# Residual tiles fetched two ahead in three buffers, and products ordered by weight half within a chunk, in a two-block float32 transformer kernel

## The chip, the cores and the metric

The kernel runs on one core of one Trainium2 chip. The metric is the device time of one execution in microseconds (us); less is better. The time before is the median of three executions, 2883.99 us (2881.13 to 2885.41).

## What is computed

Two transformer-like blocks run one after the other on a sequence of 512 tokens of width 2048, all in float32. Cut to what matters here:

```python
def reference(x, mem, ..., c_2, ctx_2, ...):
    x = first_block(x, mem, ...)      # one layer: state-space scan, differential attention, memory attention
    return second_block(x, c_2, ctx_2, ...)   # two layers on 512 tokens beside a context of 256 tokens

def first_block(x, mem, ...):
    h = rmsnorm(x, norm_pre); proj = h @ w_in            # 5120 columns
    ...
    mix = jnp.concatenate([y_s, y_d, y_x], -1) @ w_out
    x = x + rmsnorm(mix, norm_post)                      # the residual that the change is about

def second_block(x, c, ctx, ...):
    for l in range(2):
        h  = rmsnorm_2(x,  norm_g[l]) * (1 + scale) + shift
        hc = rmsnorm_2(xc, norm_g[l]) * (1 + scale_c) + shift_c
        ...                                              # both go through w_in[l], attention, pooling, a Fourier mix, w_out[l]
        x  = x + gate * out
        xc = xc + gate_c * outc                          # not in the last layer
    return rmsnorm_2(x, final_norm_g)
```

## The kernel before

**Layout.** Activations lie transposed in SBUF: 16 tiles of 128 features by n tokens (n is 512 for the sequence, 256 for the memory and the context). A product of the large weights with them is made by `gemm` (line 515): one output tile of 128 features by n tokens gathers in one PSUM tile `mm` over 2048 input features. Weights come in chunks of 512 input by 128 output features (`raw`, 256 KB, by a DMA on the SP queue). One output tile takes four chunks (two in the product with `w_glu`).

**Products in two halves.** For accuracy every float32 operand is split in a high half, rounded by ScalarE (`whi` of a weight chunk, `hh` of an activation tile), and a low half, the rest, which VectorE subtracts (`wlo`, `hl`). A product of two operands is three matmuls: high by high, high weight by low activation, low weight by high activation. `mm3` (line 328) issues them in that order, and `gemm` calls it for each of the four 128-row pieces of a chunk: 12 matmuls, of which the third is the first that needs `wlo`. There are 912 chunks.

**The weight pipeline.** `wload` (475) puts the load of a chunk on SP into one of four `raw` buffers; a `raw` buffer is free when VectorE has made the `wlo` of the chunk that lay there. `wsplit` (481) issues the cast to `whi` on ScalarE and, a little later, the subtraction to `wlo` on VectorE. Both have four buffers each, and run three chunks ahead of the products.

**The order of the work.** All engines run their instructions in the order of the program text, and the program text is made by a planner: `tick` (432), called between matmuls and with a clock that advances by the estimated cost of each matmul, lets pieces of other work ("background" generators) issue their next instructions. So evaluation of finished tiles, attention, norms and the adaptive-norm products (`adaw`, `tp`) stand between the products on every engine. In `gemm` before, `tick` is called after each of the four pieces of a chunk.

**Block 1's residual.** After the product with `w_out`, the background generator `post` in `block2` (line 1716) makes the new residual stream, tile by tile for k from 0 to 15: it loads `xr` (a tile of the kernel's input `xT`, 256 KB), multiplies `X[k]` (the tile `mx`) by the norm factor `B`, adds `xr`, writes the tile to DRAM (`x1d`) and sums its squares into `acc`. The load of tile k is issued just ahead of the multiplication and the addition of tile k, into one of two buffers. Beside this, PE makes the products of the context (256 tokens) with `w2_in0`, layer 0 of block 2: the stage from about 1023 to 1185 us of the trace.

Of the kernel before, what the change touches and what calls it, by code (L numbers as in the profile page):

```python
# [22 lines left out]
N = 512  # L23
# [191 lines left out]
class Build:  # L215
# [299 lines left out]
    def gemm(self, name, mt, H, n, order, ahead=None):  # L515
        while len(self.live["mm"]) > 1 and (self.pmx is None or self.live["mx"]):
            self.tick(0.5)
        if len(self.live["mm"]) < 2:
            ps = self.t(self.pmm, "mm", [128, n], bufs=2)
            self.live["mm"].append(ps.tensor.name)  # L520
        else:
            ps = self.t(self.pmx, "mx", [128, n])
            self.live["mx"].append(ps.tensor.name)
        ks = lambda a: [order[a] * 4 + kk for kk in range(4)] if a < len(order) else []
        for a, ci in enumerate(order):
            if ahead is not None and a == 2:
                self.spawn(self.split_ahead(ahead))
            hi, lo = self.wget((name, mt, ci, n))
            while lo.tensor.name not in self.split_w:
                self.tick(0.3)  # L530
            while any(k not in H.ok for k in ks(a)):
                self.tick(0.3)
            H.need(ks(a) + (ks(a + 1) if self.wi > 1 else []))
            for kk in range(4):
                s = slice(kk * 128, kk * 128 + 128)
                self.mm3(ps, (hi[:, s], lo[:, s]), H[ci * 4 + kk],
                         a == 0 and kk == 0, a == len(order) - 1 and kk == 3)
                if kk < 3 or a < len(order) - 1:
                    self.tick()
        return ps  # L540

# [1138 lines left out]
    def block2(self):  # L1680
        nc, I = self.nc, self.I
        o4r = (2, 3, 0, 1)

        es_c = ExitStack()
        cxp = self.pool("cx1", es_c, bufs=1)
        es = ExitStack()
        pp = self.pool("post1", es, bufs=1)
        self.ada_gap = 1.3
        X = [None] * 16
        acc = self.t(pp, "acc", [128, N])  # L1690
        hc = [self.t(cxp, f"cx{k}", [128, NC]) for k in range(KT)]
        HC = Lazy(self, NC, lambda Hk, k: self.conv(Hk, hc[k], bias=self.adav[0][:, 1, k:k + 1]), False)
        last = []

        def ev(m, ps):
            X[m] = self.t(self.xp, f"mx{m}", [128, N])
            self.act(X[m], ps, AF.Copy, scale=self.vec("norm_post", m))
            sq = acc if m == 0 else self.t(pp, "sq", [128, N], bufs=2)
            self.act(sq, ps, AF.Square)
            self.over(ps)  # L1700
            yield
            if 0 < m < 15:
                self.add(acc, acc, sq)
            last[:] = [sq]

        fs, fc = [], None
        for m, ps in self.gemms("w_out", range(16), self.H, N, o4r, HC):
            fs.append(self.spawn(ev(m, ps)))
            if m == 11:
                self.ada_until("G0_1")  # L1710
            if m == 2:
                fc = self.spawn(self.ctx_rows(hc, pp, lambda k: I["ctxT"][:, k], 0, HC))
        self.ada_gap = 4
        HX = Lazy(self, N, lambda Hk, k: self.conv(Hk, X[k], bias=self.adav[0][:, 0, k:k + 1]), False)

        def post():
            yield 12
            while self.alive([fc, *fs]):
                yield 0
            B0 = yield from self.g_bcast([acc, last[0]], N, D)  # L1720
            B = self.t(pp, "B", [128, N], bufs=2)
            yield
            nc.scalar.copy(B, B0)
            self.over(B0)
            yield
            xr = []
            for k in range(16):
                xr.append(self.t(pp, "xr", [128, N], bufs=2))
                self.load(xr[k], I["xT"][:, k])
                if k == 0:  # L1730
                    yield
                self.mul(X[k], X[k], B)
                self.add(X[k], X[k], xr[k])
                yield 3.0
                nc.sync.dma_start(out=self.x1d[k], in_=X[k])
                sq = acc if k == 0 else self.t(pp, "sq", [128, N], bufs=2)
                self.act(sq, X[k], AF.Square)
                yield 0.3
                if 0 < k < 15:
                    self.add(acc, acc, sq)  # L1740
            B0 = yield from self.g_bcast([acc, sq], N, D)
            B = self.t(pp, "B", [128, N], bufs=2)
            yield
            nc.scalar.copy(B, B0)
            self.over(B0)
            yield
            for k in list(range(8, 16)) + list(range(8)):
                self.stt(X[k], X[k], self.G0_0[:, k:k + 1], B, ALU.mult, ALU.mult)
                HX.ok.add(k)
                yield 2.2  # L1750
                if k >= 8:
                    HX.need([k])

        fp = self.spawn(post())


        es_kv = ExitStack()
        kvp = self.pool("ckv", es_kv, bufs=1, side="right")
        es_p = ExitStack()
        self.ps_ = self.pool("psSc", es_p, bufs=1, space=PSUM)  # L1760
        self.pmx = self.pool("pmx", es_p, bufs=1, space=PSUM)
        self.layer(0, NC, HC, cxp, "cx", kvp, None, lambda: (self.join(fp), es.close()), None,
                   lambda _: self.lead(self.gemms("w2_in0", range(8, 12), HX, N, o4r), self.LEAD[3]))
        es_c.close()
        es_p.close()
        self.pmx = None
        self.ps_ = self.pool("psS", bufs=1, space=PSUM)


        self.ada_gap = 2  # L1770
        self.layer(0, N, HX, self.xp, "mx", kvp, self.x1d, None, self.next_kv,
                   lambda H: self.lead(self.gemms("w2_in1", range(8, 12), H, NC, o4r), self.LEAD[3]))
        es_kv.close()


        es_kv = ExitStack()
        kvp = self.pool("ckv1", es_kv, bufs=1, side="right")
        HC, HX1, fin, es_o = self.next_h

        def early():  # L1780
            yield from fin
            for k in range(8, 16):
                HX1.need([k])
                yield 0.7
        fe = self.spawn(early(), now=False)
        es_t = ExitStack()
        tp_ = self.pool("ckt", es_t, bufs=1)
        self.scp, self.scw, self.scb = tp_, NC, 4
        self.ckv = self.kv(1, NC, HC, o4r, kvp, "c", False, self.next_kv)
        kvs = self.lead(self.gemms("w2_in1", range(8, 12), HX1, N, o4r), self.LEAD[3])  # L1790
        self.join(fe, *self.kvf)
        es_t.close()
        es_o.close()
        self.layer(1, N, HX1, self.xp, "mx", kvp, self.x2d, None, kvs)
        es_kv.close()
# [407 lines left out]
```

## Time and profile before

| What | Before |
|---|---|
| median of 3 runs | 2883.99 us (2881.13 to 2885.41) |
| the profiled execution: its own time | 2885.97 us |
| its span, first to last instruction | 2884.2 us |
| mean granted TensorE clock | 0.978 of full speed |
| PE (matmuls) busy | 2740.9 us, 95%, 17390 instructions |
| PEld (weight loads) busy | 2279.8 us, 79% |
| DVE (VectorE) busy | 1664.8 us, 58% |
| ACT (ScalarE) busy | 1213.8 us, 42% |
| POOL (GpSimd) busy | 168.3 us, 6% |
| DMA moved | 412.73 MB, mean 143 GB/s |

A share of busy time is a mean over stages that differ; what ends a wait is read stage by stage. All instructions carry line 210 (L210), since one helper records every operation, so groups go by the names of tiles: `mm<-hh,wlo` is a matmul into `mm` with moving operand `hh` and weights `wlo`, `wlo<-raw,whi` the subtraction on VectorE, `mx<-mx,xr` the residual addition. SPq is the DMA queue of SyncE, on which all loads and stores of this program are issued. An entry such as "[3.0 <-DMA xr<-xT]" at the end of a row is idle time of the engine just before the instruction, and what ended it. PEclk is the granted clock of TensorE as a share of full speed.

### The profile page before, as it was taken

The page shows a single profiled execution, that of the slowest core. Times are in us where ns is not written, and L with a number is a line of the kernel's source. Part 1 is how long each engine was busy: PE and PEld are TensorE (multiplying, and loading weights), DVE is VectorE, ACT ScalarE, POOL GpSimd, SP SyncE. Part 2 cuts the span into 40 slices and gives each one's busy share as a digit, 9 for nine tenths or more (in the row PEclk, how much of TensorE's full clock was granted, in tenths as well). Part 3 has the DMA queues.
Part 4 walks back from the last instruction along what each step waited for, and adds up shares of the span by engine and source line. Part 5 has one row for each costly group of instructions (what it writes and reads, how often), then busy time and mean ns, then how long its engine had stood idle before and what let it go on. Part 6 is the DMA issues. An engine that isn't in the chain of part 4 may idle for free.

```text
span 2884.2 us, 46821 instructions
## 1 busy us (share of the span) xinstructions
PE 2740.9 (95%) x17390; PEld 2279.8 (79%) x17390; DVE 1664.8 (58%) x3696; ACT 1213.8 (42%) x2339; POOL 168.3 (6%) x338
## 2 busy tenths in 40 slices
PE   6899999999999988899999999999999999999997
PEld 5677788778777787898987888878877778888785
DVE  8756557766643366775555455555466654555433
ACT  4544335643442344544443444444344444444322
POOL 0234334000000000000000000000000000000001
PEclk9999999999999998999999999999999999999998
DMA  5445566565576666667632222225433222222343
GB/s 173 136 155 158 178 204 208 183 223 182 185 236 210 210 220 199 193 205 222 206 101 59 63 70 81 74 73 172 143 125 108 64 65 66 76 82 74 113 119 111
DMA packets 241621, 412.73 MB, mean 143 GB/s; under 512 B 35952, under 2 KB 51312, under 8 KB 241392
## 3 DMA queue, kind: packets, MB, share of 16 engines
q1 hardware_dynamic: 241392, 409.73, 45.2%
q8 instruction: 137, 2.24, 0.3%
q14 instruction: 92, 0.75, 0.1%
HBM read 382.36 MB, written 25.17 MB: 141 GB/s over the span
## 4 chain that ended last, share of the span: by engine, by line
PE 77%; issue 8%; DVE 8%; DMA 4%; ACT 2%; SPq 1%; POOL 0%; DVEq 0%; POOLq 0%; ACTq 0%
PE mm L210 62%; PE tp L210 7%; PE pv L210 4%; PE S L210 3%; DVE wlo L210 2%; DMA raw<-w_in 2%; PE V L210 2%; DVE hl L210 1%; DMA xr<-xT 1%; DMA raw<-w_out 1%; DMA raw<-w_kv 1%; DVE mx L210 1%; ACT whi L210 1%; SPq L210 1%; DVE rs_a L210 0%
## 5 line engine op out<-in xcount | busy, mean ns | idle before, releaser
L210 PE MATMUL mm<-hh,whi 128*128 128x512 f32 (+1 forms) x3648 | 1364.6, 374 | 27.4 <-ACT hh L210 23.9
L210 PE MATMUL mm<-hh,wlo 128*128 128x512 f32 (+1 forms) x3648 | 1333.2, 365 | 55.3 <-DVE wlo L210 55.3
L210 PE MATMUL mm<-hl,whi 128*128 128x512 f32 (+1 forms) x3648 | 1331.6, 365 | 8.0 <-DVE hl L210 7.5
L210 ACT CAST whi<-raw 128x512 fp32r<-128x512 f32 x912 | 563.1, 620 | 903.6 <-PE mm L210 663.9
L210 DVE TENSOR_TENSOR wlo<-raw,whi 128x512 fp32r<-128x512 f32 x912 | 622.6, 694 | 373.7 <-ACT whi L210 369.7
L210 PEld LDWEIGHTS mm<-hh,wlo 128*128 128x128 f32 x3648 | 702.4, 193 | 169.6 <-DVE wlo L210 62.2
L210 PEld LDWEIGHTS mm<-hh,whi 128*128 128x128 f32 x3648 | 702.9, 193 | 155.0 <-ACT hh L210 26.9
L210 PEld LDWEIGHTS mm<-hl,whi 128*128 128x128 f32 x3648 | 703.9, 193 | 110.8 <-DVE hl L210 13.6
L210 DVE TENSOR_TENSOR ptl<-tp,pth 128x512 fp32r<-128x512 f32 (+3 forms) x128 | 80.7, 630 | 111.7 <-ACT pth L210 111.7
L210 ACT CAST pth<-tp 128x512 fp32r<-128x512 f32 (+3 forms) x128 | 69.2, 540 | 161.7 <-PE tp L210 148.8
L210 PE MATMUL tp<-adaw,adac 128*32 128x128 f32 x3072 | 107.6, 281 | 5.1 <-DMA adaw<-ada 5.0
L210 PEld LDWEIGHTS tp<-adaw,adac 128*32 128x32 f32 x3072 | 79.8, 111 | 34.9 <-issue 24.6
L210 POOL MEMSET s<- 128x8 f32 x24 | 1.7, 106 | 1646.2 <-DVE xk9l L210 1053.5
L210 ACT COPY s<-mm 32x512 f32<-32x512 f32 (+3 forms) x124 | 66.5, 537 | 63.2 <-PE mm L210 62.0
L210 ACT ACTIVATE s<-mm 128x512 f32<-128x512 f32 (+1 forms) x80 | 41.8, 523 | 115.4 <-PE mm L210 115.4
L210 DVE TENSOR_TENSOR acc<-acc,sq 128x512 f32<-128x512 f32 (+1 forms) x70 | 44.6, 636 | 48.6 <-ACT sq L210 45.6
L210 PE MATMUL tp<-ident,P 128*128 128x128 f32 x448 | 69.2, 274 | 0.0
L210 DVE SCALAR_TENSOR_TENSOR s<-mm,vec,axial 128x512 f32<-128x512 f32 x20 | 15.0, 752 | 92.7 <-ACT s L210 92.7
L210 PEld LDWEIGHTS tp<-ident,P 128*128 128x128 f32 x448 | 56.0, 141 | 13.5
L210 POOL TENSOR_TENSOR bb<-bb,cm 128x192 f32<-128x192 f32 (+1 forms) x96 | 57.0, 594 | 7.5
L210 DVE SCALAR_TENSOR_TENSOR mx<-mm,adav,xr 128x512 f32<-128x512 f32 x32 | 24.0, 750 | 51.4 <-PE mm L210 51.4
L210 DVE SCALAR_TENSOR_TENSOR s<-s,mm 128x512 f32<-128x512 f32 (+1 forms) x48 | 28.7, 597 | 41.5 <-ACT s L210 41.1
(938 smaller groups left out, 2487.7 us busy)
## 6 DMA issues: line engine op xcount, KB each, us to landing
raw<-w_in SPq DMA_DIRECT2D x608, 256.0 KB, 2.8
adaw<-ada SPq DMA_DIRECT2D x384, 256.0 KB, 4.0
raw<-w_out SPq DMA_DIRECT2D x256, 256.0 KB, 3.0
raw<-w_kv SPq DMA_DIRECT2D x32, 256.0 KB, 3.4
mx<-xT SPq DMA_DIRECT2D x16, 256.0 KB, 4.3
bbd<-bb SPq DMA_DIRECT2D x16, 256.0 KB, 5.1
ccd<-bb SPq DMA_DIRECT2D x16, 256.0 KB, 4.9
bb<-bbd SPq DMA_DIRECT2D x8, 512.0 KB, 5.0
```

The source lines that it names most:

```text
L210: fn(*a, **kw)
```

## The change

The change has two parts. In `gemm`, the eight matmuls of a chunk that use `whi` come first (piece by piece, by `hh` and by `hl`), and the four that use `wlo` come last; `tick` is called after each of the four pieces of the first group and after every second matmul of the other, six times a chunk where it was four. In `post`, the loads of `xr` for tiles 0 and 1 are issued ahead of the loop and the load of tile k+2 in step k, into three buffers in place of two.

```diff
@@ gemm
-            for kk in range(4):
-                s = slice(kk * 128, kk * 128 + 128)
-                self.mm3(ps, (hi[:, s], lo[:, s]), H[ci * 4 + kk],
-                         a == 0 and kk == 0, a == len(order) - 1 and kk == 3)
-                if kk < 3 or a < len(order) - 1:
-                    self.tick()
+            end = a == len(order) - 1
+            for kk in range(4):
+                w = hi[:, kk * 128:kk * 128 + 128]
+                for half in range(2):
+                    self.mm(ps, w, H[ci * 4 + kk][half], a == kk == half == 0, False)
+                self.tick()
+            for kk in range(4):
+                self.mm(ps, lo[:, kk * 128:kk * 128 + 128], H[ci * 4 + kk][0], False, end and kk == 3)
+                if kk % 2 and not (end and kk == 3):
+                    self.tick()
@@ block2, post
             xr = []
+            def fetch():
+                xr.append(self.t(pp, "xr", [128, N], bufs=3))
+                self.load(xr[-1], I["xT"][:, len(xr) - 1])
+            fetch()
+            fetch()
+            yield
             for k in range(16):
-                xr.append(self.t(pp, "xr", [128, N], bufs=2))
-                self.load(xr[k], I["xT"][:, k])
-                if k == 0:
-                    yield
+                if k < 14:
+                    fetch()
                 self.mul(X[k], X[k], B)
                 self.add(X[k], X[k], xr[k])
                 yield 3.0
```

The planner turns this into a new order on every engine. Three places matter for what follows.

PE, one chunk of the context's product with `w2_in0` (the two activation tiles of a pair share a name). Before, its second to fourth pieces:

```order
L210 MATMUL mm_11960<-hh_2477_11372,whi_11914 128x256
L210 MATMUL mm_11960<-hl_2478_11373,whi_11914 128x256
L210 MATMUL mm_11960<-hh_2477_11372,wlo_11915 128x256
L210 MATMUL mm_11960<-hh_2487_11416,whi_11914 128x256
L210 MATMUL mm_11960<-hl_2488_11417,whi_11914 128x256
L210 MATMUL mm_11960<-hh_2487_11416,wlo_11915 128x256
L210 MATMUL mm_11960<-hh_2487_11416,whi_11914 128x256
L210 MATMUL mm_11960<-hl_2488_11417,whi_11914 128x256
L210 MATMUL mm_11960<-hh_2487_11416,wlo_11915 128x256
```

Now, a whole chunk:

```order
L210 MATMUL mm_12016<-hh_2482_11398,whi_11946 128x256
L210 MATMUL mm_12016<-hl_2483_11399,whi_11946 128x256
L210 MATMUL mm_12016<-hh_2482_11398,whi_11946 128x256
L210 MATMUL mm_12016<-hl_2483_11399,whi_11946 128x256
L210 MATMUL mm_12016<-hh_2487_11413,whi_11946 128x256
L210 MATMUL mm_12016<-hl_2488_11414,whi_11946 128x256
L210 MATMUL mm_12016<-hh_2487_11413,whi_11946 128x256
L210 MATMUL mm_12016<-hl_2488_11414,whi_11946 128x256
L210 MATMUL mm_12016<-hh_2482_11398,wlo_11947 128x256 x2
L210 MATMUL mm_12016<-hh_2487_11413,wlo_11947 128x256 x2
```

The first matmul that reads `wlo` was the third of the chunk and is now the ninth; the last `hl` was read by the eleventh and is now read by the eighth.

DVE, the second step of the residual (tile `mx_2120`). Before:

```order
L210 TENSOR_TENSOR mx_2120_9580<-mx_2120_9580,B_11833 128x512
L210 TENSOR_TENSOR mx_2120_9580<-mx_2120_9580,xr_12003 128x512
L210 TENSOR_TENSOR wlo_11980<-raw_11934,whi_11979 128x512
L210 TENSOR_TENSOR cv11l_11989<-tp_11990,cv11h_11988 128x256
L210 TENSOR_TENSOR wlo_12012<-raw_11974,whi_12011 128x512
```

Now:

```order
L210 TENSOR_TENSOR mx_2120_9580<-mx_2120_9580,B_11851 128x512
L210 TENSOR_TENSOR mx_2120_9580<-mx_2120_9580,xr_11900 128x512
L210 TENSOR_TENSOR wlo_12018<-raw_11970,whi_12017 128x512
L210 TENSOR_TENSOR wlo_12033<-raw_11992,whi_12032 128x512
L210 TENSOR_TENSOR cv11l_12052<-tp_12053,cv11h_12051 128x256
```

The work on DVE is the same; the buffer that the addition reads is another, whose load is found below.

SP, the queue at that place. Before:

```order
L210 DMA x1d_80<-mx_2099_9474 128x512
L210 DMA xr_12003<-xT 128x512
L210 DMA raw_12014<-w_in 128x512
L210 DMA raw_12032<-w_in 128x512
L210 DMA x1d_80<-mx_2120_9580 128x512
```

Now, from the first two loads of `xr` on:

```order
L210 DMA xr_11898<-xT 128x512
L210 DMA xr_11900<-xT 128x512
...
L210 DMA xr_11979<-xT 128x512
...
L210 DMA x1d_80<-mx_2099_9474 128x512
L210 DMA raw_12047<-w_in 128x512
L210 DMA xr_12059<-xT 128x512
L210 DMA raw_12069<-w_in 128x512
L210 DMA raw_12087<-w_in 128x512
L210 DMA raw_12127<-w_in 128x512
L210 DMA x1d_80<-mx_2120_9580 128x512
```

Tile 1 (`mx_2120`) was loaded right ahead of its own step (`xr_12003`); it now comes with tile 0 (`xr_11900`), and what stands at the old place is the load of tile 3 (`xr_12059`), which takes the buffer of tile 0.

## Rows read from the trace of the kernel before

**Rows 1.** The page, parts 1 and 4: busy time, and the chain by engine

```profile
PE 2740.9 (95%) x17390; PEld 2279.8 (79%) x17390; DVE 1664.8 (58%) x3696; ACT 1213.8 (42%) x2339; POOL 168.3 (6%) x338
...
PE 77%; issue 8%; DVE 8%; DMA 4%; ACT 2%; SPq 1%; POOL 0%; DVEq 0%; POOLq 0%; ACTq 0%
```

**Rows 2.** Waits, whole span: who waited for whom, us in total, times, longest

```profile
PE mm L210 <- DVE wlo L210: 55.3, 31, 6.1
...
PE mm L210 <- ACT hh L210: 23.9, 10, 8.6
```

**Rows 3.** Groups of PE instructions by shape: busy us, mean ns | idle before

```profile
L210 PE MATMUL mm<-hh,wlo 128*128 128x256 f32 x1024 | 303.2, 296 | 54.0 <-DVE wlo L210 54.0
```

**Rows 4.** Busy time by windows: start, residual stage, stage after it; last: PEclk, DMA, GB/s

```profile
0.00:90.00 90.00, 56.79 (x387) 52.86 (x388) 72.37 (x250) 46.89 (x99) 0.20 (x4) 0.91 0.56 177
1023.00:1185.00 162.00, 135.89 (x1192) 128.46 (x1193) 104.76 (x270) 69.55 (x157) 0.42 (x6) 0.91 0.66 214
1185.00:1320.00 135.00, 122.94 (x1183) 117.75 (x1183) 98.25 (x255) 67.49 (x145) 0.00 (x0) 0.98 0.62 193
```

**Rows 5.** Waits in the residual stage, 1023 to 1185 us

```profile
DVE mx L210 <- DMA xr<-xT: 47.4, 16, 5.5
ACT whi L210 <- DMA raw<-w_in: 32.8, 17, 4.1
...
PE mm L210 <- DVE wlo L210: 22.2, 10, 3.8
```

**Rows 6.** Timeline of one residual step, 1065.8 to 1073.5 us: start, us, engine, instruction

```profile
1065.88 0.69 DVE L210 TENSOR_TENSOR mx<-mx,B 128x512 f32<-128x512 f32 x1
...
1066.58 0.43 SPq L210 DMA_DIRECT2D xr<-xT  x1
...
1069.68 0.28 PE L210 MATMUL mm<-hh,whi 128*128 128x256 f32 x1
...
1069.80 0.28 PE L210 MATMUL mm<-hl,whi 128*128 128x256 f32 x1
1071.82 0.69 DVE L210 TENSOR_TENSOR mx<-mx,xr 128x512 f32<-128x512 f32 x1 [5.26 <-DMA xr<-xT]
1072.42 1.29 DVE L210 TENSOR_TENSOR wlo<-raw,whi 128x512 fp32r<-128x512 f32 x2
...
1073.16 0.38 PE L210 MATMUL mm<-hh,wlo 128*128 128x256 f32 x1 [3.09 <-DVE wlo L210]
```

**Rows 7.** Waits in the stage after the residual, 1185 to 1320 us

```profile
PE mm L210 <- DVE wlo L210: 7.7, 5, 3.6
...
PE mm L210 <- ACT hh L210: 4.3, 1, 4.3
```

**Rows 8.** DMA in the residual stage: total, and one issue with its median us to landing

```profile
DMA packets 19057, 34.63 MB, mean 214 GB/s; under 512 B 2111, under 2 KB 2367, under 8 KB 19041
...
xr<-xT SPq DMA_DIRECT2D x16, 256.0 KB, 4.6
```

**Rows 9.** Waits of the SP queue in the residual stage

```profile
SPq L210 <- DVE wlo L210: 72.4, 31, 5.6
...
SPq L210 <- DVE mx L210: 3.7, 2, 3.2
```

**Rows 10.** Timeline of PE in the product of 512 tokens with w_out

```profile
911.17 0.39 PE L210 MATMUL mm<-hh,wlo 128*128 128x512 f32 x1
911.40 0.39 PE L210 MATMUL mm<-hh,whi 128*128 128x512 f32 x1
```

**Rows 11.** Waits in the first 90 us

```profile
PE mm L210 <- DVE wlo L210: 20.4, 9, 6.1
```

**Rows 12.** The chain in the first 112 us, where the memory's products end

```profile
87.07 0.69 DVE bx L210
87.76 0.14 issue
87.90 1.27 PE tp L210 x10
```

**Rows 13.** Timeline of DVE where the product with w2_out0 begins

```profile
1942.53 4.91 DVE L210 SCALAR_TENSOR_TENSOR hl<-mx,hh 128x512 fp32r<-128x512 f32 x8 [3.26 <-ACT hh L210]
```

## The prediction

> **What bounds the kernel now.** The page comes first: PE is busy 95% of the span and holds 77% of the chain that ended last, DVE 8% and DMA 4% [rows 1]. So only what makes PE wait, or run slower, is worth time, and most of the kernel offers nothing. The list of waits then says which stops of PE the change can reach: 55.3 us in 31 waits for `wlo`, the low half of a weight chunk, and 23.9 us in 10 for `hh`, the high half of an activation tile [rows 2]. The groups by shape show that 54.0 of the 55.3 us stand at matmuls of 256 tokens [rows 3]: the memory's products at the start and the context's products in block 2.
>
> The windows place them. In the residual stage, 1023 to 1185 us, PE is busy 135.89 of 162 us at a granted clock of 0.91; the stage behind it has the same products and nearly as many PE instructions (1183 against 1192), and is busy 122.94 of 135 us at 0.98 [rows 4]. The waits inside the residual stage say why: DVE waits 47.4 us, 16 times, for `xr`, and PE waits 22.2 us, 10 times, for `wlo` [rows 5]. The timeline of one step joins the two: the load of `xr` is issued at 1066.58, the addition that needs it stands still for 5.26 us, the next two `wlo` stand behind it on DVE, and PE, which came to its third matmul at 1069.9, waits 3.09 us for the first of them [rows 6].
>
> **The change, part by part.** No instruction is added or taken away: the same matmuls, weight loads, splits and 16 loads of `xr`. Only their order and one buffer differ, so every term is a wait.
>
> *Loads two ahead.* Load k+2 is issued in step k. A step lasts 162 / 16, about 10 us; two steps are far above the 4.6 us that a load takes to land here [rows 8], so DVE's 47.4 us should go. What is late next? DVE needs its 104.76 us of work and 162 - 104.76 - 47.4 = 9.8 us of other idle time, 114.6 us in all; PE needs more, so PE ends the stage. I price PE by the stage behind: 1192 x 122.94 / 1183 = 123.9 us busy. For the stops that stay I take that stage's 7.7 us for `wlo` (its other 4.3 us belong to the start of the next product) [rows 7]. The stage then takes 123.9 + 7.7 = 131.6 us, **30.4 us less**. Of that, 12.0 us come from the clock (135.89 - 123.9) and 18.4 from stops (26.1 - 7.7). Bounds: 18.4 us if the clock stays at 0.91; 26.1 + 12.0 = 38.1 if no stop stays. I take 30.4, since the stage behind is the nearest row for both. The 32.8 us in which ACT waits for `raw` [rows 5] are no end here: a `raw` buffer is free when its `wlo` is made, and SP waits 72.4 us for that [rows 9], so they follow from the late `wlo`.
>
> The loads also pass SP, where the chunks' loads stand. Load k+2 takes the buffer that the addition of step k-1 frees, and would hold the queue until then. In the new order, however, the `raw` load ahead of it (for `xr_12059`, `raw_12047`) already waits for a `wlo` that stands behind that addition on DVE; so it adds no wait.
>
> *Low halves last, elsewhere.* The first matmul that needs `wlo` comes six matmuls later in the chunk: 6 x 0.12 = 0.72 us at 256 tokens [rows 6], 6 x 0.23 = 1.4 us at 512 [rows 10]. Outside the residual stage and the first 90 us there are 31 - 10 - 9 = 12 such waits, 55.3 - 22.2 - 20.4 = 12.7 us [rows 2, 5, 11]. At 0.72 us each that is 8.6 us; some are shorter than 0.72 us, so I take **6 us**, bounds 0 and 9. In the first 90 us PE waits 20.4 us, nine times [rows 11], but DVE is busy 72.37 us there [rows 4], and the chain at the end of that stage runs through DVE's sum `bx` to the `tp` that waits for it [rows 12]. A PE that waits less there arrives earlier at the same place. I take 0, bounds -3 and +6.5 (9 x 0.72).
>
> *Activation halves wanted sooner.* The last `hl` of a chunk is read by the eighth matmul instead of the eleventh. Where a product begins and its tiles are being split, PE can now wait up to three matmuls more: 7 products of 512 tokens x 0.68 us and 4 of 256 x 0.36 us, 6.2 us in all. Against that, DVE makes a low half every 4.91 / 8 = 0.61 us at such a start [rows 13], less than the 0.68 us of three matmuls but more than the 0.46 of two; so something is lost in the first chunks and little after. I take **2 us**, bounds 0 and 6.
>
> *The rest.* `whi` is free three matmuls earlier, `wlo` as late as before: no buffer is held longer. Six planner ticks a chunk in place of four shift other work on every engine; that has no row. I take 0, with the 8.6 us of the longest wait for `hh` [rows 2] as the size of one accident, either way.
>
> *The sum.* 2885.97 (the profiled execution's own time) - 30.4 - 6 - 0 + 2 = 2851.6 us. That execution stood 1.98 us above the median of the three runs, so against the median I forecast **2850 us**, some 34 us less.
>
> **The rivals.**
>
> *The clock stays low.* [...] If many short stops are enough to hold it down, only 18.4 us of the stage come back: 2883.99 - 18.4 - 6 + 2 = 2861.6 us. For it: DVE stays busy 104.76 of some 132 us, 80%, so short stops remain. Against it: the stage behind has DVE busy 98.25 of 135 us, 73%, five stops, and a clock of 0.98 [rows 4, 7]. [...]
>
> *Transfers take the place of the wait.* The same 34.63 MB must come in 132 instead of 162 us, 262 GB/s in place of 214 [rows 8]. If loads then land later, the four `raw` buffers set the pace and half of the stops stay: a stage of about 152 us, so 2883.99 - 10 - 6 + 2 = 2870 us. For it: ACT already waits 32.8 us for `raw` [rows 5]. Against it: the DMA share is 0.66 [rows 4], and 69.55 us of ACT's work with all 32.8 us of that wait are 102 us, below 131.6.
>
> *The SP queue is held (slower).* Should a load of `xr` reach SP before the addition of step k-1 is done, it holds all `raw` loads behind it, `whi` and `wlo` come late, and PE stops. Of the 14 loads in the loop 13 reuse a buffer. The longest hold of SP by `mx` today is 3.2 us [rows 9]; 13 x 3.2 = 41.6 us would eat the gain of 34 and give 2883.99 - 34.4 + 41.6 = 2891 us. It decides from about 3.1 us a load on ((34.4 + 5.8) / 13). Against it stands the order: SP already waits for `wlo` (72.4 us in 31 waits [rows 9]), and those stand behind the additions in question.
>
> *Nothing happens in the stage.* The loads of `xr` might be issued earlier in the program and yet reach SP no sooner, with SP behind its `wlo` waits; then only the low halves count: 2883.99 - 6 + 2 = 2880 us. The order speaks against it: the second load comes with the first, some ten loads earlier in the queue.
>
> **How the numbers follow.** Forecast 0.72, clock 0.10, transfers 0.08, nothing 0.05, queue held 0.05. The range: the low end takes the upper bounds, 2883.99 - 38.1 - 9 - 6.5 = 2830 us; the high end takes in the clock and transfer rivals and ends at 2872 us. A measurement of this kernel can tell about 0.2%, 5.8 us, from no change. The first three cases lie below 2878.2 us: faster 0.90, same 0.05, slower 0.05.
>
> **What would show it.** In the changed profile the row of DVE's wait for `xr` should fall from 47.4 us in 16 to under 5; the wait of PE for `wlo` from 55.3 to about 30 us; the window of the residual stage should be near 132 us at a clock near 0.98; the stage behind should stay at 135 or lose some 4 us. Waits for `hh` and `hl` should grow by 2 to 6 us. A residual stage above 145 us, or a loss of over 8 us in a stage that the change names nowhere, would make the prediction wrong.

## The result, and the profile after

The changed kernel takes **2838.53 us** (median of four runs, 2830.89 to 2841.33), against 2883.45 us (2881.13 to 2885.41, four runs) for the kernel before: a ratio of **0.9846, 95% interval 0.983 to 0.9862**. The profiled execution took 2837.88 us with a span of 2836.1 us at a mean granted clock of 0.984; the span before was 2884.2 us. That is 48.1 us less in the profiled executions and 44.9 us between the medians, where 34 were forecast.

Busy time and the chain by engine, from the page of the kernel after; they answer to [rows 1]:

```profile
PE 2728.3 (96%) x17390; PEld 2263.2 (80%) x17390; DVE 1668.2 (59%) x3696; ACT 1207.4 (43%) x2339; POOL 159.7 (6%) x338
...
PE 79%; issue 8%; DVE 6%; DMA 3%; ACT 2%; POOL 0%; SPq 0%; POOLq 0%; ACTq 0%; DVEq 0%
```

The instruction counts are the same. PE's busy time fell by 12.6 us (2740.9 - 2728.3), which with equal matmuls goes with the higher mean clock (0.978 before, 0.984 now); the other 35.5 us of the 48.1 are stops of PE.

The waits of the kernel after, whole span (who waited for whom, us in total, times, longest); they answer to [rows 2], but for the second, which is new in this length:

```profile
DVE wlo L210 <- PE mm L210: 239.8, 161, 2.8
...
PE mm L210 <- DVE wlo L210: 24.2, 16, 4.7
PE mm L210 <- ACT hh L210: 23.3, 12, 8.6
...
PE pv L210 <- DVE ptl L210: 2.8, 4, 0.7
...
DVE mx L210 <- DMA xr<-x1d: 2.0, 1, 2.0
```

The row of `mx` waiting for `xr<-xT` (47.4 us in 16 [rows 5]) is gone; a single wait for another `xr`, of 2.0 us, is what is left of its name. PE's waits for `wlo` fell from 55.3 to 24.2 us. The row of `pv` and `ptl` matters below. The 239.8 us in which DVE now waits for a `wlo` buffer that PE still reads (1.0 us before) are no loss in themselves: DVE is early there.

Windows of the kernel after (stretch, its length, busy time of PE, PEld, DVE, ACT and POOL with instruction counts, then PEclk, DMA share, GB/s): the first 90 us, the residual stage, the stretch behind it, and the product of 512 tokens with `w2_in0`. The first three answer to [rows 4]; the residual stage is cut as before, 8 us ahead of the first addition of `xr` to 7 us behind the last one's start:

```profile
0.00:90.00 90.00, 61.79 (x412) 57.68 (x412) 70.34 (x243) 46.51 (x99) 0.20 (x4) 0.91 0.57 179
1025.00:1157.00 132.00, 121.64 (x1156) 115.03 (x1156) 107.37 (x286) 69.33 (x158) 0.41 (x6) 0.99 0.78 251
1157.00:1288.40 131.40, 122.79 (x1157) 118.84 (x1156) 97.14 (x243) 66.87 (x142) 0.00 (x0) 0.99 0.63 196
1388.70:1899.70 511.00, 507.91 (x2458) 416.84 (x2456) 279.97 (x592) 214.62 (x391) 0.55 (x8) 1.00 0.27 79
```

The residual stage lasts 132.0 us at a clock of 0.99, where it took 162 at 0.91. It holds 36 matmuls fewer (1156 against 1192), so its 26.1 us without PE at work have become 10.4.

Where the time went over the whole kernel is read by cutting both traces at the first matmul of each product, which are the same 10,944 matmuls in every kernel here (us; the runs are told of below):

| From the first matmul of one product to that of the next | before | after | loads ahead alone | + new order, 4 ticks | + old order, 6 ticks | mixed |
|---|---|---|---|---|---|---|
| `w_kv` (memory) | 86.8 | -6.7 | -1.5 | -7.1 | -3.3 | -7.0 |
| `w_in` | 644.9 | +9.8 | +0.2 | -2.9 | +5.0 | -0.9 |
| `w_glu`, `w_out` | 258.8 | +1.6 | 0.0 | -0.1 | +1.0 | -0.3 |
| context, layer 0 (holds the residual) | 421.3 | -36.3 | -25.7 | -26.5 | -41.0 | -30.1 |
| `w2_in0` (attention, layer 0) | 522.2 | -11.2 | -4.0 | +2.8 | -11.2 | -8.1 |
| `w2_out0`, context of layer 1 | 215.0 | -0.1 | -1.0 | -1.1 | -0.9 | -1.2 |
| `w2_in1` (attention, layer 1) | 525.9 | -4.9 | +2.9 | +4.4 | -5.2 | -7.9 |
| `w2_out1` to the end | 200.7 | -0.2 | -0.1 | -0.4 | 0.0 | -0.2 |
| span | 2884.2 | -48.1 | -29.7 | -31.2 | -55.0 | -55.2 |

Each column comes from one trace. The kernel after and the one with six ticks in the old order were traced a second time (runs 10 and 11 below): the attention stages came within 0.9 us of the first trace, the context stage of layer 0 within 3.6, the other rows within 1.7. Differences below that tell nothing.

Three things were not in the forecast: the start is 6.7 us shorter, `w_in` 9.8 longer, and the two attention stages, where the prediction expected next to nothing, 16.1 shorter together. The first two largely cancel: the first output tile of `w_in` takes 20.5 us where it took 13.4, and its second one begins at 109.1 us of the trace, where it began at 108.8. (The planner also moved 64 matmuls of the adaptive norms from the context stage of layer 0 to beside `w_in`, `w_glu` and `w_out`; 3072 of them keep PE busy for 107.6 us in the kernel before, so 64 are some 2.2 us. The attention stages hold as many matmuls as before, 2456 and 2458.)

### The profile page after: what moved, and what is told of

Its sections match the earlier page's. It is cut to its first block, busy times and chain, and to the rows that moved or that the text cites. A ratio compares the mean times of both kernels' runs of the same rounds, so it can differ in the third digit from the quotient of the medians.

```text
span 2836.1 us, 46799 instructions
## 1 busy us (share of the span) xinstructions
PE 2728.3 (96%) x17390; PEld 2263.2 (80%) x17390; DVE 1668.2 (59%) x3696; ACT 1207.4 (43%) x2339; POOL 159.7 (6%) x338
## 4 chain that ended last, share of the span: by engine, by line
PE 79%; issue 8%; DVE 6%; DMA 3%; ACT 2%; POOL 0%; SPq 0%; POOLq 0%; ACTq 0%; DVEq 0%
PE mm L210 64%; PE tp L210 7%; PE pv L210 4%; PE S L210 2%; PE V L210 2%; DMA raw<-w_in 2%; DVE wlo L210 1%; DVE hl L210 1%; DVE mx L210 1%; ACT whi L210 1%; DMA raw<-w_kv 1%; DMA xr<-xT 0%; ACT hh L210 0%; DMA raw<-w_out 0%; DVE e_p L210 0%
## 5 line engine op out<-in xcount | busy, mean ns | idle before, releaser
L210 PE MATMUL mm<-hh,whi 128*128 128x512 f32 (+1 forms) x3648 | 1317.8, 369 | 34.7 <-ACT hh L210 23.3
L210 PE MATMUL mm<-hl,whi 128*128 128x512 f32 (+1 forms) x3648 | 1301.0, 365 | 7.0 <-DVE hl L210 6.2
L210 PE MATMUL mm<-hh,wlo 128*128 128x512 f32 (+1 forms) x3648 | 910.9, 367 | 24.3 <-DVE wlo L210 24.2
L210 DVE TENSOR_TENSOR wlo<-raw,whi 128x512 fp32r<-128x512 f32 x912 | 624.5, 695 | 358.4 <-PE mm L210 239.8
L210 PEld LDWEIGHTS mm<-hh,wlo 128*128 128x128 f32 x3648 | 634.0, 191 | 136.6 <-DVE wlo L210 28.3
L210 ACT COPY s<-mm 32x512 f32<-32x512 f32 (+3 forms) x124 | 66.4, 536 | 55.3 <-PE mm L210 54.1
L210 PEld LDWEIGHTS tp<-ident,P 128*128 128x128 f32 x448 | 56.0, 141 | 13.8 <-issue 0.2
L210 DVE TENSOR_TENSOR adaa<-adaa,tp 128x128 f32<-128x128 f32 x72 | 20.5, 285 | 58.4 <-PE tp L210 58.0
```

Of the source, the lines that this page charges most:

```text
L210: fn(*a, **kw)
```

## What stood in the attention stages

The timeline of the kernel before, in the product of 512 tokens with `w2_in0` (start, us, engine, instruction, and in brackets the idle time before it):

```profile
1519.07 0.59 ACT L210 CAST pth<-tp 128x512 fp32r<-128x512 f32 x1 [2.08 <-PE tp L210]
...
1519.57 0.40 PE L210 MATMUL mm<-hh,whi 128*128 128x512 f32 x1
1519.81 0.40 PE L210 MATMUL mm<-hl,whi 128*128 128x512 f32 x1
...
1521.08 2.34 ACT L210 COPY s<-mm 32x512 f32<-32x512 f32 x4
1521.32 0.48 PE L210 MATMUL pv<-pth,cv10h 128*128 128x512 f32 x1
1523.45 0.75 DVE L210 SCALAR_TENSOR_TENSOR s<-mm,vec,axial 128x512 f32<-128x512 f32 x1 [5.69 <-ACT s L210]
1524.12 0.68 DVE L210 TENSOR_TENSOR ptl<-tp,pth 128x512 fp32r<-128x512 f32 x1
1524.85 0.79 PE L210 MATMUL pv<-ptl,cv10h 128*128 128x512 f32 x1 [3.05 <-DVE ptl L210]
...
1525.87 0.63 PE L210 MATMUL mm<-hh,whi 128*128 128x512 f32 x1
1526.30 0.63 PE L210 MATMUL mm<-hl,whi 128*128 128x512 f32 x1
```

`pth` and `ptl` are the halves of a tile of attention weights. `pth` was ready at 1519.66, so `ptl` could have been made then. But DVE had come to `s<-mm,vec,axial`, a step of the rotary embedding (`g_rope`), ahead of it, and this waits for four copies on ScalarE (2.34 us), themselves behind a step that waited 0.81 us for PE. `ptl` comes next on DVE, at 1524.12, so it starts 4.5 us late and PE stands 3.05 us.

The stop is not all: behind it, matmuls start every 0.43 us (1525.87, 1526.30) where they started every 0.23 or 0.24 (1519.57, 1519.81). The windows of the kernel before show the clock for it, 1.00 ahead of the stop and 0.58 in the seven us behind it (the third line is the whole product):

```profile
1510.00:1520.00 10.00, 10.00 (x47) 7.92 (x46) 4.29 (x9) 4.14 (x8) 0.00 (x0) 1.00 0.39 107
1525.00:1532.00 7.00, 7.00 (x21) 5.35 (x21) 2.95 (x5) 1.01 (x2) 0.00 (x0) 0.58 0.12 41
1420.40:1942.60 522.20, 514.00 (x2458) 420.79 (x2457) 280.12 (x592) 215.68 (x391) 0.56 (x8) 0.99 0.26 78
```

There are two such stops in each layer. The row of the waits of the kernel before that gathers them:

```profile
PE pv L210 <- DVE ptl L210: 12.4, 4, 3.1
```

In the kernel after, the stretch around the same rotary step reads:

```profile
1487.25 0.59 ACT L210 CAST pth<-tp 128x512 fp32r<-128x512 f32 x1 [1.89 <-PE tp L210]
...
1487.87 0.69 DVE L210 TENSOR_TENSOR ptl<-tp,pth 128x512 fp32r<-128x512 f32 x1 [1.69 <-ACT pth L210]
...
1489.95 2.35 ACT L210 COPY s<-mm 32x512 f32<-32x512 f32 x4
...
1492.10 1.07 PE L210 MATMUL mm<-hh,wlo 128*128 128x512 f32 x4
...
1492.33 0.75 DVE L210 SCALAR_TENSOR_TENSOR s<-mm,vec,axial 128x512 f32<-128x512 f32 x1 [3.77 <-ACT s L210]
...
1494.26 0.68 DVE L210 TENSOR_TENSOR ptl<-tp,pth 128x512 fp32r<-128x512 f32 x1
...
1495.00 0.50 PE L210 MATMUL pv<-ptl,xv10h 128*128 128x512 f32 x1 [0.71 <-DVE ptl L210]
```

Three `ptl` of this group now stand ahead of the rotary step on DVE, where one did, so the tile that is held up is the fourth (its matmul reads `xv10h`) and no longer the second (`cv10h`). PE has products to do while DVE waits (the four matmuls at 1492.10 are some of them), and the stop is 0.71 us. The clock does not fall there: it is 1.00 from 1495 to 1502 us, and the whole product of 512 tokens is at 1.00 (last row of the windows above), with 507.91 us of PE for the same 2458 matmuls that took 514.00.

So three parts had to be told apart: the loads, the order of the matmuls in a chunk, and the number of ticks.

## The experiments

All ratios are against the kernel before on the same chip.

### 1. The loads two ahead alone

```diff
@@ post, as in the change (gemm as before)
-                xr.append(self.t(pp, "xr", [128, N], bufs=2))
-                self.load(xr[k], I["xT"][:, k])
...
+                if k < 14:
+                    fetch()
```

> The change's loads alone: xr two ahead in three buffers, the products of a chunk in the old order with four ticks. Theory A (the forecast's: DVE's wait for xr is what stops PE in the residual stage, the order of the products is worth little there): the product of the context with w2_in0 takes 290 us instead of 319.7, DVE's wait for xr falls under 5 us, and the whole is 2883 - 30 = 2853 us. Theory B (the late low halves need the new order too: without it DVE, 80% busy, still stops PE at the third matmul of a chunk): that product takes 305 us and the whole is about 2868 us.

Measured: 2853.39 us (2848.41 to 2857.33) against 2881.18, ratio 0.9896 [0.9872, 0.9919]. The context's product with `w2_in0`, beside which the residual stands, is 28.0 us shorter than its 319.7; the start moved by 1.5 us, and the four attention stops stand as before (PE's wait of `pv` for `ptl`: 12.5 us in 5, of which four are over 3 us).

### 2. The order and the six ticks alone

```diff
@@ gemm, as in the change (post as before)
-                self.mm3(ps, (hi[:, s], lo[:, s]), H[ci * 4 + kk],
...
+                for half in range(2):
+                    self.mm(ps, w, H[ci * 4 + kk][half], a == kk == half == 0, False)
+                self.tick()
...
```

> The change's order of products alone (eight by whi, then four by wlo, six ticks), xr loaded as before. Theory A: the residual stage keeps DVE's 47 us of waiting for xr and nearly all its stops of PE (10 waits, each shorter by 0.7 us at most, so 5 to 7 us less); with the 18 us that the changed kernel gained behind that stage and the 5 us that it lost ahead of it, the whole is 2883 - 6 - 18 + 5 = 2864 us. Theory B (order and loads help only together): 2875 us or more.

Measured: 2867.99 us (2866.78 to 2868.78), ratio 0.995 [0.9932, 0.9967]. The residual waits for `xr` as ever; the row of the waits:

```profile
DVE mx L210 <- DMA xr<-xT: 50.5, 16, 6.4
```

The context stage of layer 0 is only 5.2 us shorter, but the attention stages are shorter by 11.2 and 4.6 and the start by 6.8, and `w_in` is longer by 7.2 (its second output tile begins at 107.3 us): every move of the changed kernel that the loads do not make. The two parts add up: 0.9896 x 0.995 = 0.9847, against 0.9846 measured for both.

### 3. The loads and the new order, four ticks a chunk

```diff
@@ gemm, against the kernel before
-                self.mm3(ps, (hi[:, s], lo[:, s]), H[ci * 4 + kk],
...
+            jobs = [(hi, kk, half) for kk in range(4) for half in range(2)] + [(lo, kk, 0) for kk in range(4)]
+            for i, (w, kk, half) in enumerate(jobs):
+                self.mm(ps, w[:, kk * 128:kk * 128 + 128], H[ci * 4 + kk][half],
+                        a == i == 0, end and i == 11)
+                if i % 3 == 2 and not (end and i == 11):
+                    self.tick()
```

> The change with the planner's ticks left where they were: xr two ahead, eight products by whi and then four by wlo, but a tick after every third product. Theory O (what the changed kernel gained in the later products of 512 tokens, 11.2 us in w2_in0 and 4.9 in w2_in1, is the order of the products): these gains stay, 2840 us. Theory T (it is the planner's other placing of attention work, which six ticks bring): they are gone, w2_in0 takes 522 us as before with its two stops of 3.3 us at the attention products, and the whole is about 2850 us; the 13.8 us that the product with w_in lost at the start are gone as well under T.

Measured: 2854.33 us (2849.32 to 2855.83), ratio 0.9897 [0.9876, 0.9917], the same as with the loads alone. PE's waits for `wlo` did fall, from 37.5 us in 26 to 29.5 in 15, and `w_kv` is 5.6 us shorter than there (-7.1 against -1.5). But this is no time gained: the second output tile of `w_in` begins at 107.0 us in this kernel and at 106.8 with the loads alone. The rest of `w_in` is 8.8 us shorter than there, and the attention stages are longer by about as much (+2.8 and +4.4 for -4.0 and +2.9); 64 matmuls of the adaptive norms have moved from the one to the other. The stops of attention are there (12.6 us in 5).

### 4. The loads and six ticks a chunk, old order

```diff
@@ gemm, against experiment 3
-            jobs = [(hi, kk, half) for kk in range(4) for half in range(2)] + [(lo, kk, 0) for kk in range(4)]
+            jobs = [x for kk in range(4) for x in ((hi, kk, 0), (hi, kk, 1), (lo, kk, 0))]
...
-                if i % 3 == 2 and not (end and i == 11):
+                if i % 2 and not (end and i == 11):
                     self.tick()
```

> xr two ahead and six ticks a chunk, but the old order of products (by hh, by hl, by wlo, piece by piece), a tick after every second product. Theory T: the gains of 11.2 us in w2_in0 and 4.9 us in w2_in1 are here without the new order, 2842 us or so. Theory O: they are not, and the whole is 2853 us as with the loads alone.

Measured: 2830.91 us (2829.16 to 2838.87), ratio 0.9824 [0.9801, 0.9847]. Without the new order the kernel is at least as fast as the change. DVE has three `ptl` ahead of the rotary step, as in the kernel after; the timeline of this kernel:

```profile
1481.75 0.69 DVE L210 TENSOR_TENSOR ptl<-tp,pth 128x512 fp32r<-128x512 f32 x1 [1.29 <-ACT pth L210]
...
1486.21 0.75 DVE L210 SCALAR_TENSOR_TENSOR s<-mm,vec,axial 128x512 f32<-128x512 f32 x1 [3.77 <-ACT s L210]
...
1488.88 0.50 PE L210 MATMUL pv<-ptl,xv10h 128*128 128x512 f32 x1 [0.71 <-DVE ptl L210]
```

Of its 25.3 us of span below the loads alone, 15.3 lie in the two attention stages. The context stage of layer 0 shows 15.3 more, but part of that is work done elsewhere: it holds 160 matmuls of the adaptive norms fewer (3308 against 3468), which now stand beside `w_in` (96 more) and `w_glu` and `w_out` (64 more), and these stages are 5.8 us longer. The rest of that stage's gain goes with fewer stops of PE of over 1 us in the context's `w2_in0` (five in place of nine); what removed each of them was not tried.

### 5. The loads one ahead, two buffers

```diff
@@ post, against experiment 1
-                xr.append(self.t(pp, "xr", [128, N], bufs=3))
+                xr.append(self.t(pp, "xr", [128, N], bufs=2))
...
-            fetch()
             fetch()
             yield
...
-                if k < 14:
+                if k < 15:
```

> The loads alone, one tile ahead in two buffers instead of two tiles ahead in three; products and ticks as before. A step of the residual lasts 8 to 10 us and a load lands in 4.6 us, so if latency is all there is to it, one ahead is enough: no wait for xr over 5 us in total, and 2853 us as with two ahead. If the load is held up on the SP queue behind loads of raw (which wait for wlo), one ahead is too short: DVE still waits 10 to 20 us for xr and the whole is 2860 us or more.

Measured: 2853.26 us (2852.42 to 2861.33), ratio 0.9907 [0.9882, 0.9932], with the old order and four ticks. The wait for `xr` is all but gone with the old two buffers:

```profile
DVE mx L210 <- DMA xr<-xT: 3.0, 2, 1.7
```

One step ahead is enough; the third buffer and the second step bring nothing that is measured here.

### 6. The rotary copies in two pieces (with the loads alone)

```diff
@@ g_rope
         for j in range(4):
             d = 32 * (j ^ 1)
             nc.scalar.copy(sw[d:d + 32, :], src[32 * j:32 * j + 32, :])
+            if j == 1:
+                yield
```

> xr two ahead, the old order of products and four ticks (as the loads alone), and the four rotary copies of ScalarE issued two and two, with a yield of the planner between. Theory R (the four stops of 3.3 us at attention products, two in each layer, come from a cast of attention that stands behind all four copies, 2.34 us, on ScalarE; six ticks only moved it): with other work let in between, the stops fall under 1.5 us each and the two layers' products with w2_in gain 8 to 16 us, 2840 to 2845 us in all. Rival (the stops hang on where the ticks fall, not on the copies): the stops stay near 3.3 us and the whole is 2853 us or more.

Measured: 2842.51 us (2841.38 to 2844.42), ratio 0.9864 [0.9843, 0.9885], at the old four ticks and in the old order: 10.9 us less than with the loads alone by the medians, 9.2 by the ratios ((0.9896 - 0.9864) x 2883). Of the experiments it comes closest to a direct test of the stop, since only the rotary piece is cut; but the cut is also one more place where the planner lets other work in, and two `ptl` now stand ahead of the step where one did, so the two theories above are not fully parted. Theory R names the wrong engine: what stands behind the copies is not a cast on ScalarE but `ptl` on DVE, which waits behind the rotary step, and that one waits for the copies. Its timeline around the same rotary step:

```profile
1492.20 0.69 DVE L210 TENSOR_TENSOR ptl<-tp,pth 128x512 fp32r<-128x512 f32 x1 [1.92 <-ACT pth L210]
...
1493.59 1.16 ACT L210 COPY s<-mm 32x512 f32<-32x512 f32 x2
...
1495.91 1.17 ACT L210 COPY s<-mm 32x512 f32<-32x512 f32 x2
...
1497.11 0.75 DVE L210 SCALAR_TENSOR_TENSOR s<-mm,vec,axial 128x512 f32<-128x512 f32 x1 [4.22 <-ACT s L210]
...
1499.12 0.51 PE L210 MATMUL pv<-ptl,xv10h 128*128 128x512 f32 x1 [0.94 <-DVE ptl L210]
```

`w2_in0` and `w2_in1` are 10.6 and 5.5 us below before, as with six ticks. `w_in` is 7.0 above it, where `g_rope` is used too: the gain in one place comes with a loss in another.

### 7. A tick after every matmul

```diff
@@ gemm, against experiment 4
-                if i % 2 and not (end and i == 11):
+                if not (end and i == 11):
                     self.tick()
```

> xr two ahead, the old order of products, a tick after every product (12 a chunk). If finer ticks are better as such (work is let in when it is due, not up to three products late), this is at or below the 2831 us of six ticks. If six ticks were a lucky placing of a few pieces of attention work, twelve give anything between 2830 and 2860 us, and the stops stand at other places.

Measured: 2837.31 us (2834.37 to 2842.75), ratio 0.9847 [0.9824, 0.9871]. Attention keeps its gain (-10.1 and -6.2), but `w_in` is 20.1 us longer. More ticks are not better as such.

### 8. The new order in the memory's product alone, six ticks

```diff
@@ gemm, against experiment 4
-            jobs = [x for kk in range(4) for x in ((hi, kk, 0), (hi, kk, 1), (lo, kk, 0))]
+            if name == "w_kv":
+                jobs = [(hi, kk, half) for kk in range(4) for half in range(2)] + [(lo, kk, 0) for kk in range(4)]
+            else:
+                jobs = [x for kk in range(4) for x in ((hi, kk, 0), (hi, kk, 1), (lo, kk, 0))]
```

> xr two ahead, six ticks, the new order of products in the first product (w_kv, 256 tokens of memory) alone, the old order everywhere else. With the new order and four ticks that product was 5.6 us shorter and the gain was kept to the end of block 1. If it is kept here too: 2831 - 3 to 5 = 2827 us. If the product with w_in gives it back, as in the changed kernel (13.8 us lost there): 2831 us or more.

Measured: 2832.14 us (2829.3 to 2832.85), ratio 0.9826 [0.98, 0.9851]. `w_kv` is 6.7 us shorter, as in the change, and `w_in` 7.3 longer. Against experiment 4 `w_kv` gained 3.4 us, but the second output tile of `w_in` begins at 107.0 us, where it began at 105.3 there: nothing is kept, as forecast for the second case.

### 9 to 11. A mixed version beside the change and beside six ticks in the old order

```diff
@@ gemm, against experiment 4
+            two = name.startswith("w2_")
+            if two:
+                jobs = [x for kk in range(4) for x in ((hi, kk, 0), (hi, kk, 1), (lo, kk, 0))]
+            else:
+                jobs = [(hi, kk, half) for kk in range(4) for half in range(2)] + [(lo, kk, 0) for kk in range(4)]
...
+                if i % (2 if two else 3) == (1 if two else 2) and not (end and i == 11):
```

> Edit: the loads of xr two ahead; in block 1's products the new order with four ticks a chunk, in block 2's the old order with six. Theory A (each half of the program keeps its own gain, since what matters is which piece of background work meets which product): block 1 as in the run with the new order and four ticks (w_kv -7.1, w_in -0.8 and -2.1, w_glu and w_out -0.1, 10 us less than before), block 2 as in the run with six ticks in the old order (-33.6, -7.4, -11.2, -1.6, +0.8, -5.2, 58 us less): a span of 2816 us, below every kernel so far. Rival B (the accidents are drawn anew by any change of the program, so sums of stages from two kernels do not hold): 2825 to 2840 us, with stops at new places.

> No edit: the change once more, on the chip of the two other runs, for their comparison. Expected 2831 to 2841 us.

> No edit: the loads of xr two ahead and six ticks a chunk in the old order once more, on the same chip as the change. Theory T (the new order of the products brings nothing, the ticks do): not above the change, 2829 to 2836 us. Rival (the new order brings something of its own): over 5.8 us (0.2%) above the change.

Measured on one chip:

| Kernel | Median (range), us | Ratio [95%] |
|---|---|---|
| mixed | 2828.53 (2824.39 to 2830.76) | 0.9823 [0.9805, 0.9841] |
| the change | 2834.52 (2831.7 to 2835.15) | 0.9844 [0.9827, 0.9861] |
| six ticks, old order | 2831.24 (2830.47 to 2834.29) | 0.9837 [0.9819, 0.9854] |

The mixed version has the lowest median of all, 6.0 us below the change on the same chip, just over the 5.8 us that a measurement can tell, and its range lies below the change's; the intervals of the ratios overlap. Against six ticks in the old order (2.7 us, and 0.9824 in experiment 4) it can't be told apart. A span of 2816 us was expected and 2829.0 came. The front half came out as summed (-8.2 for -10); the context stage of layer 0 did not, -30.1 for -41.0, in part since the adaptive norms' 160 matmuls stayed in it (3468 matmuls, as in the run with the new order and four ticks; some 5.6 us by the 107.6 us of 3072), and PE also stands idle for 24.9 us there instead of 18.4 in experiment 4. `w2_in0` holds 64 matmuls more. Stages of two kernels do not simply add: the front half decides what is left to do in the back half. Six ticks in the old order are 3.3 us below the change here, within the 5.8 us that a measurement can tell, so the order is worth nothing or costs a little. (The second output tile of `w_in` begins at 105.6 us in this trace and at 109.4 in that of the change, as in experiment 4 and the first trace of the change, 105.3 and 109.1.)

## Why the prediction was right, and where it was not

**The whole.** 2838.53 us against 2850, inside the range. The gain was 11 us larger than forecast, and the parts that make it up differ from those of the forecast. The loads alone give 2853 us, so the mechanism that carried the forecast carries most of the result too. The rest is luck: the 6 us expected of the order did not come, and a term that was priced at nothing, the ticks, brought more than that.

*Loads two ahead, -30.4.* Right in mechanism and close in size. Alone they take 27.8 us off the median (experiment 1), and on top of the rest 29.5 (2867.99 - 2838.53, from two sets of runs). The clock came back, 0.91 to 0.99, and the wait for `xr` is gone. The stage itself took 132.0 us for 131.6 forecast; at its own 0.105 us a matmul (121.64 / 1156) the 36 matmuls that it lacks are another 3.8, so 26 us of 30 for equal work. Not all of that belongs to the loads: with the loads alone, the stage cut the same way (1021.1 to 1138.6 us, 982 matmuls) has a clock of 0.97 and PE still waits 9.7 us in 8 for `wlo`, near the 7.7 us that the forecast allowed. What is late next shows in the waits of the kernel after, 1025 to 1157 us, beside [rows 5]:

```profile
ACT whi L210 <- DMA raw<-w_in: 35.1, 21, 5.5
...
PE mm L210 <- DVE wlo L210: 1.6, 3, 0.8
```

PE hardly waits for `wlo` any more (1.6 us for 22.2). ScalarE's wait for `raw`, which the prediction took to follow from the late `wlo`, stayed (35.1 us for 32.8). The timeline of the largest stop that is left in the stage:

```profile
1060.03 0.69 DVE L210 TENSOR_TENSOR mx<-mx,xr 128x512 f32<-128x512 f32 x1
1060.42 1.28 ACT L210 CAST whi<-raw 128x512 fp32r<-128x512 f32 x2 [5.32 <-DMA raw<-w_in]
...
1061.60 0.47 ACT L210 ACTIVATE cx<-mm,vec 128x256 f32<-128x256 f32 x1
...
1062.12 0.39 PE L210 MATMUL mm<-hh,whi 128*128 128x256 f32 x1 [3.21 <-ACT cx L210]
```

The addition waits for nothing, but ScalarE waited 5.32 us for a chunk, the evaluation `cx<-mm` stands behind its casts, and PE stands 3.21 us until `cx` has read the finished tile out. The loads of `xr` still land 4.7 us after their issue (4.6 before [rows 8]) at 251 GB/s, so the rival in which transfers take the place of the wait did not come; nor did the held queue, with SP's waits for `mx` at 3.9 us in 2 in the stage (3.7 in 2 [rows 9]).

*The clock rival.* It did not come: the stage stands at 0.99, although DVE is busy 107.37 of 132 us and PE's short stops remain, 10.4 us in all. With 26.1 us of stops, before, the stage stood at 0.91. In attention, the clock was 1.00 over the seven us behind each of the four stops of 0.69 to 0.71 us in the kernel after, and 0.57 to 0.76 behind three of the four of some 3.1 us in the kernel before. What sets the clock in a stage with stops was not shown.

*Low halves last elsewhere, -6, and the start, 0.* The first failed, the second held. The low halves do make PE wait less for `wlo` (37.5 to 29.5 us, experiment 3), but that is no time gained: with four ticks the order moves the median by +0.9 us, with six by +3.3 on one chip. At the start the table shows 6.7 us less for `w_kv`, but only because of where it is cut. The `tp` that waits for `bx` was moved, from 87.9 us [rows 12] behind the next product's first chunks, so `w_in` begins earlier and PE is stopped inside its first output tile instead. The first matmul of `w_in`'s second output tile before, and now with the stop ahead of it:

```profile
108.77 0.39 PE L210 MATMUL mm<-hh,whi 128*128 128x512 f32 x1
```

```profile
107.54 0.65 PE L210 MATMUL tp<-bx,ones 128*32 128x128 f32 x8 [2.65 <-DVE bx L210]
...
109.14 0.63 PE L210 MATMUL mm<-hh,whi 128*128 128x512 f32 x1
```

PE that waits less arrives earlier at the place where it waits for DVE, as the prediction said. With six ticks in the old order the same point is reached at 105.3 us, so there the new order costs 3.8 us.

*Activation halves wanted sooner, +2.* It did not come: the waits of PE for `hh` went from 23.9 to 23.3 us, for `hl` from 7.5 to 6.2. The four-tick pair says the same (23.2 and 8.1 us without the order, 23.1 and 8.1 with it). PE's longest stop of this kind, 8.6 us, is the same before and after.

*The rest, 0 with 8.6 for an accident.* This is the mis-sized step. Six ticks in place of four were worth 0.9824 against 0.9896, 22.5 us of the median between experiments 1 and 4; of the 25.3 us between their spans, 15.3 are in attention. Their row existed: PE's 12.4 us in 4 waits for `ptl` stands in the same list of waits from which [rows 2] come, and the lines behind it would have shown what stood ahead of `ptl` on DVE. A tick is where other work enters the queues, so its number sets which piece stands ahead of which. The opposite accident is there as well: `w_in` is 9.8 us longer (13.8 in its first part, less 3.9 in the second). 7.1 us of it are its first output tile, told above; another 5.7 lie in one output tile (280.6 to 306.8 us, before 280.2 to 300.7). Three rows of the timeline of the kernel after show four copies of the same form, now in block 1, in the way there (before, PE stood 3.24 us near this point, for another tile):

```profile
280.92 2.34 ACT L210 COPY r_t<-mm 32x512 f32<-32x512 f32 x4
...
283.29 0.69 DVE L210 TENSOR_TENSOR r_t<-mm,mx 128x512 f32<-128x512 f32 x1 [3.57 <-ACT r_t L210]
...
286.36 0.47 PE L210 MATMUL tp<-ident,mx 128*128 128x128 f32 x1 [4.83 <-DVE mx L210]
```

By the prediction's own words a loss of over 8 us in a stage that the change names nowhere would have spoken against it. By the cut at the first matmul `w_in` shows such a loss; counted from its second output tile on it is 2.7 us, so whether the sign was given hangs on the cut. Counted so, the new order with four ticks makes `w_in` 8.6 us shorter than before, six ticks in the old order 5.6 longer, and the two together 2.7 longer (1.6 without the loads), with 64 fewer, 96 more and 32 more matmuls of the adaptive norms beside it.

**Its signs.** Wait for `xr` under 5: gone. Wait for `wlo` about 30: 24.2. Stage near 132 us at 0.98: 132.0 at 0.99. The stage behind, -4 at most: 131.4 for 135, with 26 matmuls fewer. Waits for `hh` and `hl` +2 to +6: -1.9, wrong.

What stays open: why the rest of `w_in` is 8.8 us shorter with the new order and four ticks than with the loads alone, what removed the context's stops with six ticks, and whether a set of tick positions exists that keeps every gain at once.

## What to carry to other kernels

Look for a load that is issued just ahead of its use on an engine that others wait for: here such loads, 4.6 us each to landing, made DVE wait 47.4 us in 16, and behind one such wait of 5.26 us PE stood 3.09 us for `wlo` [rows 5, 6]; one step ahead already brought DVE's wait to 3.0 us in 2 and the ratio to 0.9907 (two steps: 0.9896). Where a planner mixes work into a product, count a change of its call points as a change of the program: list PE's waits for every releaser, small ones too, and look at what stands ahead of that releaser on its engine before pricing it at nothing. Try to cut an instruction run that waits (here four copies and the step behind them) into pieces, so that short work with a waiting consumer can get ahead of it, and look at every stage for what that moves elsewhere. And when a stage looks shorter, see whether a point some way into the next stage is reached earlier too.

## What the runs showed of the hardware that was not expected

A stop of 3.05 us in a stretch of dense matmuls at a clock of 1.00 was followed, in the kernel before, by matmuls at 0.43 us each where they took 0.23: from 1525.45 to 1530.93 us thirteen matmuls of 512 columns took 5.5 us, some 2.5 more than at 0.23. By this estimate that stop cost nearly twice its length. But a stop of this length was not always followed by a lower clock. Of the four (3.05 to 3.13 us), the clock was lower behind three (0.58, 0.57 and 0.76 over the seven us behind them); behind the one of 3.06 us that ends at 2269.77, at the same point of layer 1, it was 1.00:

```profile
2270.00:2277.00 7.00, 7.00 (x40) 5.34 (x40) 5.18 (x16) 1.73 (x3) 0.00 (x0) 1.00 0.27 75
```

What decides between the two was not tried. Behind the stops of 0.71 us (kernel after) and of 0.94 us (experiment 6) around the same rotary step the clock was 1.00.
